# Second norm of a hybrid decoder layer: its small products get fixed places between the large ones

## The chip, the cores and the metric

The kernel runs on one NeuronCore of a Trainium2 chip. The metric is the device time of one execution in microseconds. The engines are named as in the profile: PE (TensorE matmul), PEld (TensorE weight load), DVE (VectorE), ACT (ScalarE), POOL (GpSimd) and SP (SyncE, whose queue issues most transfers).

## The reference

One layer over a prompt of 2048 tokens and eight single-token samples, `D_MODEL` 1024, `D_FF` 2816, all float32. What surrounds the change, cut to its core:

```python
h = rmsnorm(x, g_mix) * (1.0 + scale_m) + shift_m          # first norm
proj = h @ w_in                                            # q, k, v, gate, two LRU branches
...                                                        # retention heads, RG-LRU block
mix = jnp.concatenate([ret_out, lru_out], axis=-1) @ w_out # output projection
x = x + gate_m * mix

h = rmsnorm(x, g_ffn) * (1.0 + scale_f) + shift_f          # second norm
u = h @ w_up_conv
gv = h @ w_up_gate
uc, s_conv_ffn_new = causal_dwconv(u, s_conv_ffn, conv_ffn_w, conv_ffn_b)
f = (jax.nn.gelu(uc) * gv) @ w_down
x = x + gate_f * f
```

`rmsnorm` divides each token's row by the root of its mean square; then a final norm gives the output.

## The kernel before, in words

The 2056 columns (2048 tokens and 8 samples) are worked in three groups, each cut into two blocks of 344 or 340 columns (688 with the samples in the last group). Activations lie with features on the partitions, eight tiles of 128 features (`KC` = 8), and tokens along the free axis. Every large product is made three times in reduced float32: high part by high part, high by low, low by high (`mm3`; its three matmuls are lines 373, 374 and 375 in the profile). A "product" here is twelve such matmuls of 128 x 128 by 344 columns.

The program is a list of items (`group_items`), each with the weight blocks that it needs, a rate and a function. The main loop fetches weight blocks a little ahead, runs the function, and then advances two lists of generators: `soon` (by the item's rate) and `bg`. Instructions are traced in this order; a planner that models the engines' times then orders each engine's queue by readiness and priority. `urgent` wraps a generator so that its instructions get a priority ahead of their place. PSUM has two pools: `psm` with three banks and `pst` with five.

The end of a group's first half is the output projection `out_((2, 3), apart, 2)`: eight items for the first block, one for each feature tile, then eight for the second. An item makes one product (`down_item`, tile `down`), and VectorE adds it, scaled, to `x` (line 851). ScalarE squares each new tile of `x` (line 873) and VectorE adds the squares up (line 877); the last square of a block stays apart. Then `norm2` of the block is put into `soon`:

- the sums over features: for each piece of 128 tokens two small products, of the running sum and of the last square, with a column of ones (tile `bc`, line 888);
- mean and epsilon on VectorE (line 892), the power -1/2 on POOL (894), one diagonal tile for each piece on VectorE (897);
- the broadcast of the factor to all partitions by a product of ones and the diagonal tile (899);
- the operands of the FFN: `operands1` for the first block (`scaled` at line 913 and `hilo` at 923 and 924, tile by tile), `operands2` for the second.

The FFN's up-projections are made by a Strassen scheme with seven products on 2 x 2 halves. The two token blocks are its column halves. `PRODUCTS` names for each product the weight part and the operand: P1 takes `b11` and P2 `b21`, which come from the first block alone; P5 takes `t1`, P6 `t2`, P3 `b22`, P7 `t3`, P4 `t4`, which need the second block too. The accumulating PSUM banks are called `qx`, `qy` and `qz`. A quad is one such set for one pair of feature tiles and one of `w_up_conv` and `w_up_gate`. After the output projection come the P1 and P2 of quad 0 for both matrices, then the P1 and P2 of three further quads (`early`), then the rest of quad 0, in the order P5, P6, P3, P7, P4. `keep` copies a bank out of PSUM (`p`, line 1016, or with an addition line 1101).

Before the next group, `norm1` of that group makes its diagonal tiles (line 564) and broadcasts them (line 566).

Of the kernel before, what the change touches and what calls it, by code (L numbers as in the profile page):

```python
# [2 lines left out]

# [1 line left out]

# [9 lines left out]
ALU = mybir.AluOpType  # L15

P = 128
D = 1024
KC = D // P
# [79 lines left out]
def hybrid_step(ctx: ExitStack, tc: tile.TileContext, I, O):  # L99
# [35 lines left out]
    def tiny(cols, name):  # L135
        if cols == P:
            return sp.tile([P, P], F32, tag="wide", name=name, bufs=WIDE)
        return sp.tile([P, cols], F32, tag=name, name=name, bufs=1 if cols > 32 or name[:3] == "sp_" else None)
# [10 lines left out]
    ident = cst[:, C_ID:C_ID + P]  # L149
# [116 lines left out]
    units = {}  # L266
# [74 lines left out]
    def fetch_operand(key, lo_on):  # L341
# [25 lines left out]
        if (i == 1 or i == 2 and kind == "w_up_conv") and nm in ("A11", "A12"):  # L367

            del pr[nm]

    def mm3(out, wh, wl, xh, xl, first, last, more=False):

        T.matmul(out, wh, xh, start=first, stop=False, skip_group_check=more)  # L373
        T.matmul(out, wh, xl, start=False, stop=False, skip_group_check=more)  # L374
        T.matmul(out, wl, xh, start=False, stop=last, skip_group_check=more)  # L375

    ada_ps = {}

# [53 lines left out]
    def urgent(gen, offset=HASTE):  # L432

        while True:
            with tc.high_priority(offset=offset):
                try:
                    next(gen)
                except StopIteration:
                    return
            yield  # L440
# [33 lines left out]
    class Group:  # L474
# [83 lines left out]
        def norm1(g, b, how):  # L558
            bc = pst("bc") if g.gi else psm("bc")
            for i, (c0, w) in enumerate(g.pieces):  # L560
                a0, a1 = max(c0, b[0]), min(c0 + w, b[1])
                if a0 < a1:
                    dg = tiny(P, "dg")
                    V.tensor_scalar(out=dg[0:w, 0:a1 - a0], in0=ident[0:w, a0 - c0:a1 - c0],
                                    scalar1=g.r1[i][0:w, 0:1], scalar2=None, op0=ALU.mult)
                    T.matmul(bc[:, a0 - b[0]:a1 - b[0]], ones[0:w, :], dg[0:w, 0:a1 - a0],
                             start=True, stop=True)
            yield
            yield from g.hnorm(b, bc, 1, 0, how)
# [272 lines left out]
        def down_item(g, keys, parts, jg, b, m):  # L842

            np_, n = g.npr(b), b[1] - b[0]
            q = psm("down")
            for i, key in enumerate(keys):
                wh, wl = (v[:, m % 4, :] for v in units[key])
                xh, xl = parts[i][b]
                mm3(q[:, 0:n], wh, wl, xh, xl, i == 0, i == len(keys) - 1)
            xs = g.xk(m)[:, b[0]:b[0] + np_]  # L850
            V.scalar_tensor_tensor(out=xs, in0=q[:, 0:np_], scalar=modv[:, jg, m, 0:1], in1=xs,  # L851
                                   op0=ALU.mult, op1=ALU.add)
            if np_ < n:
                if (jg, m) not in g.started:
                    g.started.add((jg, m))
                    V.tensor_copy(fsv[:, m, :], q[:, np_:n])
                else:
                    V.tensor_tensor(out=fsv[:, m, :], in0=fsv[:, m, :], in1=q[:, np_:n], op=ALU.add)
# [19 lines left out]

        def norm2(g, b):
            n = b[1] - b[0]  # L880
            acc, sq = g.sq.pop(b)
            bc = pst("bc2")
            z = bc[:, 512 - 16:512]

            pcs = [(i, min(i, n - P), min(P, n - i)) for i in range(0, n, P)]
            for i, (_, r0, _) in enumerate(pcs):
                for a in (acc, sq):
                    T.matmul(z[:, 2 * i:2 * i + 2], a[:, r0:r0 + P], ones[:, 0:2],
                             start=(a is acc), stop=(a is sq))
            ss = tiny(8, "ss2")  # L890
            k = len(pcs)
            V.tensor_scalar(out=ss[:, 0:k], in0=z[:, 0:2 * k].rearrange("p (i t) -> p i t", t=2)[:, :, 0],
                            scalar1=1.0 / D, scalar2=EPS, op0=ALU.mult, op1=ALU.add)
            G.tensor_tensor(out=ss[:, 4:4 + k], in0=ss[:, 0:k], in1=mhalf[:, 0:k], op=ALU.pow)
            for i, (c0, r0, w) in enumerate(pcs):
                dg = tiny(P, "dg")
                V.tensor_scalar(out=dg[:, 0:w], in0=ident[:, c0 - r0:c0 - r0 + w],
                                scalar1=ss[:, 4 + i:5 + i], scalar2=None, op0=ALU.mult)
                T.matmul(bc[:, c0:c0 + w], ones, dg[:, 0:w], start=True, stop=True)
            yield  # L900
            yield from (g.operands1 if b == g.blocks[0] else g.operands2)(b, bc)

# [24 lines left out]
        def operands1(g, b, bc):  # L927
            g.n = n = b[1] - b[0]
            g.op = {v: slot("op", F32R) for v in ("b11", "b21")}
            g.keep32 = slot("keep")  # L930
            for k in range(KC):
                g.scaled(k, b[0], n, bc, g.raw32(k))
                g.hilo("b11" if k < 4 else "b21", k % 4, g.raw32(k), modv[:, 3, k, 0:1])
                yield

        def raw32(g, k):
# [65 lines left out]
        def product(g, st, key, nm, bank, start, tile):  # L1002

            wh, wl = units.pop(key)
            if start:
                st[bank] = tile("q" + bank)
            q = st[bank][:, 0:g.n]
            for k in range(4):
                mm3(q, wh[:, k, :], wl[:, k, :], g.hi(nm, k), g.lo(nm, k), start and k == 0, k == 3, not start)
            return q  # L1010

        def keep(g, q, name, more=None, pool=None):
# [8 lines left out]
        def quad_item(g, st, kind, i, what, out, apart):  # L1021

            left, right, bank, start = PRODUCTS[what]
            if apart:
                bank = "y" if what in ("P1", "P2") else bank
                start = what in ("P1", "P5", "P6")
            q = g.product(st, (kind, i, left), right, bank, start,
                          psm if bank == "y" and i < 3 else pst)
            p1 = st.get("p1")
            if what == "P1":  # L1030
                st["p1"] = g.keep(q, "p1", pool=fp if i == 1 else None)
            elif what == "P5":
                st["p5"] = g.keep(q, "p5", p1 if apart else None)
            elif what == "P6":
                st["u2"] = g.keep(q, "u2", p1 if apart else None)
            elif what == "P2":
                out(2 * i, 0, q, None if apart else st.pop("p1"))
            elif what == "P7":
                out(2 * i + 1, 1, q, st.pop("p5"))
            elif what == "P3":  # L1040
                out(2 * i, 1, q, st.pop("u2"))
            else:
                out(2 * i + 1, 0, q, st.pop("p1") if apart else None)
# [151 lines left out]
    def group_items(g, nxt):  # L1195
# [3 lines left out]
        def add(keys, rate, fn, *a):  # L1199
            out.append((keys, rate, fn, a))  # L1200
# [20 lines left out]
        def out_(ps, order, rate):  # L1221

            rows_, its, had = [512 * i + P * p for p in ps for i in range(2)], [], None

            def item(b, m, ks, norm):
                while any(b not in g.mixt.get(q, {}) for p in ps for q in (p, 4 + p)):
                    advance(bg)
                g.down_item(ks, [g.mixt[q] for p in ps for q in (p, 4 + p)], 2, b, m)
                if not norm:
                    return  # L1230
                if g.npr(b) < b[1] - b[0]:
                    g.gate_samples(2, m, 1)
                past = g.past.setdefault(b, [])
                past.append(m)
                if len(past) > 1:
                    g.square(b, past[-2], False)
                if len(past) == KC:
                    g.square(b, m, True)
                    soon.append(urgent(g.norm2(b)))

            for b, m in order:
                ks = [("w_out", a, m // 4) for a in rows_]
                its.append(([] if had == m // 4 else ks, rate, item, (b, m, ks, H - 1 in ps)))
                had = m // 4
            return its

        quads = {}

        def quad(kind, i, what, rate=1):
            st = quads.setdefault((kind, i), {})  # L1250
# [31 lines left out]
        lru(2)  # L1282
        lru(3)
        head(3, True)
        out.extend(out_((2, 3), apart, 2))
        its, out[n:] = out[n:], []

        ahead = [(kind, 0, nm) for kind in (UP, GATE)
# [3 lines left out]
        for it in its:  # L1292
            out.append(it)
            due += 0.45 * min(it[1], 1)
            if ahead and due >= 1:
                due -= 1
                key = ahead.pop(0)
                add([key], 0, units.pop, key)
        for kind in (UP, GATE):
            for what in ("P1", "P2"):  # L1300
                quad(kind, 0, what, 3)
        for what in ("P1", "P2"):
            for kind, i in early:
                quad(kind, i, what, 3)
        add([], 0, lambda: drain(soon))
        for pair in (("P5",), ("P6",), ("P3",), ("P7", "P4")):
            for kind in (UP, GATE):
                for what in pair:
# [144 lines left out]
```

## Time and profile before

| | |
|---|---|
| median of 3 runs | 2462.89 us (2462.57 to 2464.89) |
| profiled execution, its own time | 2463.86 us |
| its span | 2462.1 us |
| mean granted TensorE clock | 0.988 |
| PE busy | 2359.8 us (96%) |
| PEld busy | 2275.5 us (92%) |
| DVE busy | 1452.9 us (59%) |
| ACT busy | 869.6 us (35%) |
| POOL busy | 716.9 us (29%) |
| moved by DMA | 536.04 MB, mean 218 GB/s |

Busy time is counted inside the span, from the first to the last instruction of the profiled execution. Matmuls are pipelined: a record lasts about 0.32 us, while the next one starts about 0.16 us after it. A row of the trace's timeline gives the start, the length, engine, line, operation, tile written and tiles read, and in brackets how long the engine stood idle before it and what released it.

### The profile page before, as it was taken

What the parts mean: (1) busy time and instruction counts of PE and PEld (TensorE: products, weight loads), DVE (VectorE), ACT (ScalarE), POOL (GpSimd) and SP (SyncE); (2) the same over time, 40 slices, a digit from 0 to 9 for tenths busy, and PEclk for the clock granted to TensorE, in tenths of its full rate; (3) what the DMA queues carried; (4) which work ended last, traced back from release to release, by engine and by line L of the source; (5) the groups of instructions that cost most, each with busy time, mean ns of one, the idle gap of its engine ahead of it and who ended that gap; (6) DMA issues with size and microseconds to landing.
All of it is one profiled execution on the core that took longest, in us unless ns stands there. A gap on an engine that the chain in (4) does not pass through costs nothing.

```text
span 2462.1 us, 40114 instructions
## 1 busy us (share of the span) xinstructions
PE 2359.8 (96%) x15157; PEld 2275.5 (92%) x15157; DVE 1452.9 (59%) x3181; ACT 869.6 (35%) x1964; POOL 716.9 (29%) x739
## 2 busy tenths in 40 slices
PE   5999998999999999999899999999999989999998
PEld 4987797999999999999899999999999989999998
DVE  5646777875766665666754444446667675444444
ACT  4323554544444444243422222243124241222222
POOL 3444440257666743243001010112222210101011
PEclk9999999999999999999999999999999999999999
DMA  9476655878878875343566666666442465666674
GB/s 299 163 261 223 210 172 190 305 276 287 304 285 304 323 251 184 120 157 139 189 222 235 222 238 220 241 213 215 139 130 96 145 231 199 239 220 234 219 252 160
DMA packets 243493, 536.04 MB, mean 218 GB/s; under 512 B 19223, under 2 KB 114055, under 8 KB 243292
## 3 DMA queue, kind: packets, MB, share of 16 engines
q1 hardware_dynamic: 242220, 532.01, 62.6%
q8 instruction: 120, 1.97, 0.3%
q10 hardware_dynamic: 696, 0.91, 0.1%
q0 software_dynamic: 384, 0.56, 0.1%
q14 instruction: 73, 0.60, 0.1%
HBM read 385.10 MB, written 148.42 MB: 217 GB/s over the span
## 4 chain that ended last, share of the span: by engine, by line
PE 53%; DVE 4%; ACT 2%; DMA 1%; issue 1%; POOL 1%; POOLq 0%; SPq 0%; ACTq 0%; DVEq 0%
PE down L374 6%; PE down L373 6%; PE down L375 6%; PE qx L374 4%; PE qx L375 4%; PE qx L373 4%; PE proj L373 3%; PE proj L375 3%; PE proj L374 3%; PE qz L373 2%; PE qz L374 2%; PE qz L375 2%; PE qy L374 1%; PE qy L373 1%; PE qy L375 1%
## 5 line engine op out<-in xcount | busy, mean ns | idle before, releaser
L851 DVE SCALAR_TENSOR_TENSOR x<-down,mod,x 128x344 f32<-128x344 f32 (+2 forms) x624 | 349.0, 569 | 347.0 <-PE down L375 342.3
L373 PE MATMUL proj<-hh,wb 128*128 128x344 f32 (+1 forms) x1152 | 378.5, 329 | 14.3 <-DVE h L580 6.0
L375 PE MATMUL proj<-hh,wb 128*128 128x344 f32 (+1 forms) x1152 | 373.6, 325 | 2.7 <-POOL wb L304 2.5
L374 PE MATMUL proj<-hl,wb 128*128 128x344 f32 (+1 forms) x1152 | 372.5, 323 | 0.0
L458 POOL TENSOR_TENSOR ffl<-cv,ffh 128x344 fp32r<-128x344 f32 (+1 forms) x120 | 124.7, 1046 | 782.0 <-ACT ffh L457 736.7
L374 PE MATMUL qx<-op,wb 128*128 128x344 f32 (+1 forms) x1020 | 325.5, 319 | 2.6 <-DVE op L921 2.6
L373 PE MATMUL qx<-op,wb 128*128 128x344 f32 (+1 forms) x1020 | 324.7, 320 | 1.2 <-ACT op L920 1.2
L375 PE MATMUL qx<-op,wb 128*128 128x344 f32 (+1 forms) x1020 | 324.5, 319 | 0.0
L373 PE MATMUL down<-ffh,wb 128*128 128x344 f32 (+1 forms) x960 | 304.7, 324 | 7.6 <-DVE x L851 7.4
L375 PE MATMUL down<-ffh,wb 128*128 128x344 f32 (+1 forms) x960 | 306.4, 319 | 0.0
L374 PE MATMUL down<-ffl,wb 128*128 128x344 f32 (+1 forms) x960 | 306.3, 319 | 0.0
L304 POOL TENSOR_TENSOR wb<-wr,wb 128x512 fp32r<-128x512 f32 x164 | 223.9, 1376 | 230.7 <-ACT wb L303 222.1
L373 PEld LDWEIGHTS proj<-hh,wb 128*128 128x128 f32 x1152 | 218.4, 190 | 25.9 <-issue 9.5
L375 PEld LDWEIGHTS proj<-hh,wb 128*128 128x128 f32 x1152 | 218.7, 190 | 5.7 <-POOL wb L304 3.9
L374 PEld LDWEIGHTS proj<-hl,wb 128*128 128x128 f32 x1152 | 219.1, 190 | 3.3 <-POOL hl L588 0.9
L1076 DVE SCALAR_TENSOR_TENSOR cv<-u,vec,cv 128x344 f32<-128x344 f32 (+2 forms) x264 | 170.8, 665 | 50.6 <-ACT cv L1056 48.1
L374 PEld LDWEIGHTS qx<-op,wb 128*128 128x128 f32 x1020 | 191.7, 188 | 3.4 <-DVE op L921 3.4
L373 PEld LDWEIGHTS qx<-op,wb 128*128 128x128 f32 x1020 | 191.5, 188 | 2.0 <-ACT op L920 1.8
L373 PEld LDWEIGHTS down<-ffh,wb 128*128 128x128 f32 x960 | 179.3, 188 | 14.3 <-DVE x L851 13.7
L375 PEld LDWEIGHTS qx<-op,wb 128*128 128x128 f32 x1020 | 191.4, 188 | 0.0
L373 PE MATMUL qz<-op,wb 128*128 128x344 f32 (+1 forms) x528 | 169.7, 325 | 14.6 <-ACT op L920 10.7
L375 PEld LDWEIGHTS down<-ffh,wb 128*128 128x128 f32 x960 | 180.6, 188 | 0.0
(314 smaller groups left out, 4952.1 us busy)
## 6 DMA issues: line engine op xcount, KB each, us to landing
wb<-w_down SPq DMA_DIRECT2D x100, 512.0 KB
wb<-w_up_conv_S SPq DMA_DIRECT2D x92, 512.0 KB
wb<-w_up_gate_S SPq DMA_DIRECT2D x92, 512.0 KB
wb<-w_in SPq DMA_DIRECT2D x72, 512.0 KB
wb<-w_up_conv_A SPq DMA_DIRECT2D x69, 512.0 KB
wb<-w_up_gate_A SPq DMA_DIRECT2D x69, 512.0 KB
w_in<-wb SPq DMA_DIRECT2D x48, 512.0 KB
w_up_conv_S<-wb SPq DMA_DIRECT2D x44, 512.0 KB
```

The lines of the kernel that those rows point to most:

```text
L304: lo_on.tensor_tensor(out=w[:, 512:1024], in0=src, in1=w[:, 0:512].bitcast(F32), op=ALU.subtract)
L373: T.matmul(out, wh, xh, start=first, stop=False, skip_group_check=more)
L374: T.matmul(out, wh, xl, start=False, stop=False, skip_group_check=more)
L375: T.matmul(out, wl, xh, start=False, stop=last, skip_group_check=more)
L458: G.tensor_tensor(out=lo[:, 0:n], in0=src, in1=hi[:, 0:n].bitcast(F32), op=ALU.subtract)
L851: V.scalar_tensor_tensor(out=xs, in0=q[:, 0:np_], scalar=modv[:, jg, m, 0:1], in1=xs, op0=ALU.mult, op1=ALU.add)
L1076: V.scalar_tensor_tensor(out=cv[:, 0:np_], in0=u[:, j:j + np_], scalar=cfw[:, j, ft:ft + 1], in1=cv[:, 0:np_], op0=ALU.mult, op1=ALU.add)
```

## The change

1. All eight squares of a block go into one running sum on VectorE, so the sums take one small product for each piece of 128 tokens.
2. `norm2` no longer goes into `soon` but into a list of its own, `chain`, advanced by step items at given positions: its sums stand after one more product, its broadcast after another, and then one operand tile is made with each item. The rate of the output projection's items goes from 2 to 1.
3. Ordering edges without a semaphore (`issue_after`) tie the small products behind the last large product traced (`last_mm`), all later large products of `down_item` and `product` behind the last small product (`hold`), the operand instructions on VectorE (and the first norm's diagonal tiles) behind the last addition to `x` (`last_add`), and the first products on `t1` behind the last early product.
4. The early products come by halves: P1 of quad 0 for both matrices, then P2 of both, then the six early ones. For the second block the sums stand after the first P1, the broadcast after the second, and the operand steps after the others, three for each.
5. The `qy` bank of quad 0 comes from `pst` instead of `psm`.

```diff
+    last_mm, last_add, hold = [None], [None], [None]
+    def behind(ref):
+        return tc.issue_after(ref[0].ins) if ref[0] is not None else nullcontext()
...
-        T.matmul(out, wl, xh, start=False, stop=last, skip_group_check=more)
+        last_mm[0] = T.matmul(out, wl, xh, start=False, stop=last, skip_group_check=more)
... norm1
-                    V.tensor_scalar(out=dg[0:w, 0:a1 - a0], in0=ident[0:w, a0 - c0:a1 - c0],
-                                    scalar1=g.r1[i][0:w, 0:1], scalar2=None, op0=ALU.mult)
+                    with behind(last_add):
+                        V.tensor_scalar(out=dg[0:w, 0:a1 - a0], in0=ident[0:w, a0 - c0:a1 - c0],
+                                        scalar1=g.r1[i][0:w, 0:1], scalar2=None, op0=ALU.mult)
... down_item
-            for i, key in enumerate(keys):
-                wh, wl = (v[:, m % 4, :] for v in units[key])
-                xh, xl = parts[i][b]
-                mm3(q[:, 0:n], wh, wl, xh, xl, i == 0, i == len(keys) - 1)
+            with behind(hold):
+                for i, key in enumerate(keys):
+                    wh, wl = (v[:, m % 4, :] for v in units[key])
+                    xh, xl = parts[i][b]
+                    mm3(q[:, 0:n], wh, wl, xh, xl, i == 0, i == len(keys) - 1)
...
-            V.scalar_tensor_tensor(out=xs, in0=q[:, 0:np_], scalar=modv[:, jg, m, 0:1], in1=xs,
-                                   op0=ALU.mult, op1=ALU.add)
+            last_add[0] = V.scalar_tensor_tensor(out=xs, in0=q[:, 0:np_], scalar=modv[:, jg, m, 0:1], in1=xs,
+                                                 op0=ALU.mult, op1=ALU.add)
... norm2
-            acc, sq = g.sq.pop(b)
+            acc, = g.sq.pop(b)
...
-            for i, (_, r0, _) in enumerate(pcs):
-                for a in (acc, sq):
-                    T.matmul(z[:, 2 * i:2 * i + 2], a[:, r0:r0 + P], ones[:, 0:2],
-                             start=(a is acc), stop=(a is sq))
+            with behind(last_mm):
+                for i, (_, r0, _) in enumerate(pcs):
+                    hold[0] = T.matmul(z[:, 2 * i:2 * i + 2], acc[:, r0:r0 + P], ones[:, 0:2], start=True, stop=True)
...
+            dgs = []
             for i, (c0, r0, w) in enumerate(pcs):
-                dg = tiny(P, "dg")
-                V.tensor_scalar(out=dg[:, 0:w], in0=ident[:, c0 - r0:c0 - r0 + w],
+                dgs.append(tiny(P, "dg"))
+                V.tensor_scalar(out=dgs[i][:, 0:w], in0=ident[:, c0 - r0:c0 - r0 + w],
                                 scalar1=ss[:, 4 + i:5 + i], scalar2=None, op0=ALU.mult)
-                T.matmul(bc[:, c0:c0 + w], ones, dg[:, 0:w], start=True, stop=True)
+            yield
+            with behind(last_mm):
+                for i, (c0, r0, w) in enumerate(pcs):
+                    hold[0] = T.matmul(bc[:, c0:c0 + w], ones, dgs[i][:, 0:w], start=True, stop=True)
             yield
... operands1
-                g.scaled(k, b[0], n, bc, g.raw32(k))
-                g.hilo("b11" if k < 4 else "b21", k % 4, g.raw32(k), modv[:, 3, k, 0:1])
+                with behind(last_add):
+                    g.scaled(k, b[0], n, bc, g.raw32(k))
+                    g.hilo("b11" if k < 4 else "b21", k % 4, g.raw32(k), modv[:, 3, k, 0:1])
... product
-            for k in range(4):
-                mm3(q, wh[:, k, :], wl[:, k, :], g.hi(nm, k), g.lo(nm, k), start and k == 0, k == 3, not start)
+            with behind(hold), behind(last_mm if nm == "t1" and key[1] == 0 else [None]):
+                for k in range(4):
+                    mm3(q, wh[:, k, :], wl[:, k, :], g.hi(nm, k), g.lo(nm, k), start and k == 0, k == 3, not start)
... quad_item
-                          psm if bank == "y" and i < 3 else pst)
+                          psm if bank == "y" and 1 <= i < 3 else pst)
... out_
-                    g.square(b, m, True)
-                    soon.append(urgent(g.norm2(b)))
+                    g.square(b, m, False)
+                    chain.append(urgent(g.norm2(b)))
...
+        def steps(n):
+            add([], 0, lambda: [advance(chain) for _ in range(n)])
...
-        out.extend(out_((2, 3), apart, 2))
+        for i, it in enumerate(out_((2, 3), apart, 1)):
+            out.append(it)
+            if i >= KC:
+                steps(2 if i == KC + 1 else 2 if i == 2 * KC - 1 else 1)
...
-        for kind in (UP, GATE):
-            for what in ("P1", "P2"):
-                quad(kind, 0, what, 3)
-        for what in ("P1", "P2"):
-            for kind, i in early:
-                quad(kind, i, what, 3)
-        add([], 0, lambda: drain(soon))
+        first = [(kind, 0, what) for what in ("P1", "P2") for kind in (UP, GATE)]
+        first += [(kind, i, what) for what in ("P1", "P2") for kind, i in early]
+        for n, v in enumerate(first):
+            quad(*v)
+            steps(1 if n < 2 else 3)
+        add([], 0, lambda: drain(chain))
```

More of the change, by code (lines that the diff above doesn't have):

```diff
@@ L1 @@
 import math
-from contextlib import ExitStack
+from contextlib import ExitStack, nullcontext
 import numpy as np
@@ L1245, in out_ @@
             return its
-        quads = {}
+        chain, quads = [], {}
+        def steps(n):
+            add([], 0, lambda: [advance(chain) for _ in range(n)])
         def quad(kind, i, what, rate=1):
```

## The prediction

> **What bounds the kernel now.** I read the page first, then TensorE's idle time by windows, then its waits, then the instructions in order of time around the second norm.
>
> ```profile
> span 2462.1 us, 40114 instructions
> PE 2359.8 (96%) x15157; PEld 2275.5 (92%) x15157; DVE 1452.9 (59%) x3181; ACT 869.6 (35%) x1964; POOL 716.9 (29%) x739
> ```
>
> TensorE (PE) is the bound: only 102 us of the span are idle, and nothing else is above 59%. A change can win only idle PE time, PE time at reduced clock, or PE work. The three stretches from the last output-projection product of a group to the end of its first FFN products, one per token group:
>
> ```profile
> 386.00:431.80 45.80, 34.53 (x189) 31.99 (x187) 37.05 (x83) 19.81 (x47) 3.76 (x2) 0.89 0.57 201
> 1188.00:1232.40 44.40, 37.11 (x213) 35.12 (x212) 34.03 (x77) 19.00 (x51) 4.62 (x3) 0.92 0.64 224
> 1974.00:2016.80 42.80, 35.65 (x212) 34.05 (x213) 33.97 (x97) 21.51 (x54) 3.80 (x3) 0.96 0.61 215
> sum 133.00, PE 107.29 PEld 101.16 DVE 105.04 ACT 60.33 POOL 12.18; mean PE 35.76 PEld 33.72 DVE 35.01 ACT 20.11 POOL 4.06
> ```
>
> Columns: window, length, busy PE, PEld, DVE, ACT, POOL, then granted clock, DMA share, GB/s. PE is idle 133.00 - 107.29 = 25.7 us here, a quarter of its idle time in 5% of the span. Who ends it (engine, line, released by: total us, times, longest):
>
> ```profile
> PE qz L373 <- ACT op L920: 10.7, 3, 6.3
> PE qy L373 <- ACT p L1016: 4.0, 3, 1.7
> PE qz L373 <- ACT p L1016: 3.6, 3, 2.1
> PE qx L374 <- DVE op L921: 2.6, 3, 1.2
> PE qx L373 <- ACT op L920: 1.2, 1, 1.2
> PE qy L374 <- DVE op L924: 1.1, 2, 0.6
> PE bc L888 <- DVE sq L877: 1.0, 1, 1.0
> PE qz L374 <- DVE op L921: 0.8, 2, 0.5
> ```
>
> These are 25.0 of the 25.7 us. The first is the first product on `t1`: after the second block's broadcast PE has nothing placed to run while the operand is made. In the second group:
>
> ```profile
> 1188.06 0.32 PE L373 MATMUL qy<-op,wb 128*128 128x340 f32 x1
> 1194.59 1.40 PE L888 MATMUL bc<-ones,sq 128*128 128x2 f32 x12
> 1195.84 0.40 PE L373 MATMUL qx<-op,wb 128*128 128x340 f32 x1
> 1199.68 0.79 PE L899 MATMUL bc<-dg,ones 128*128 128x128 f32 x6
> 1202.20 0.58 PE L373 MATMUL qz<-op,wb 128*128 128x340 f32 x2 [1.73 <-ACT op L920]
> ```
>
> Three early products run, then the sums, two more products (3.84 us for two: 1.9 each), the broadcast, a 1.73 us hole. The other early products come after `t1`'s, when they cover nothing. The clock also drops:
>
> ```profile
> 404.00:414.00 10.00, 6.92 (x28) 0.66 0.26 95
> 421.00:427.00 6.00, 5.60 (x26) 0.72 0.37 124
> 1203.00:1209.00 6.00, 5.87 (x27) 0.72 0.02 5
> 1227.00:1232.00 5.00, 5.00 (x23) 0.66 0.67 210
> 1988.00:1994.00 6.00, 5.45 (x23) 0.72 0.06 20
> ```
>
> (Window, length, busy PE, clock, DMA share, GB/s.) Length times (1 - clock) is the loss: 1.7 us in each of the last four. The first has 3.4, part of it under idle; I take 2.5.
>
> **The change part by part.**
>
> *Sums.* The last square joins the others on VectorE, so each piece needs one small product, not two. 12 records took 1195.84 - 1194.59 = 1.25 us, 0.104 each; 6 norms lose 6 each: **-3.75 us** of PE work. VectorE gains 6 additions of 0.5 us; they lengthen the way to the sums and are counted in the waits below. POOL's power steps stay six.
>
> *Products by halves, `t1` last.* Between the second block's broadcast and the first `t1` product now stand eight early products, 8 x 1.9 = 15 us. The operand needed 1.7 to 6.3 us. Its waits go: 10.7 + 0.8 = **-11.5**; the reduced clock behind them goes with them: 2.5 + 1.7 + 1.7 = **-5.9**. The ten weight blocks are the same in another order; SP's queue carries no transfer more, and 512 KB per 1.9 us asks 277 GB/s, so I looked at what the stretch before the broadcast already moved:
>
> ```profile
> 1181.60:1200.40 18.80, 17.75 (x116) 17.06 (x115) 13.25 (x34) 6.31 (x13) 0.85 (x1) 1.00 0.77 283
> 1200.40:1225.00 24.60, 19.78 (x109) 18.20 (x108) 24.35 (x52) 13.77 (x36) 2.87 (x1) 0.93 0.48 162
> ```
>
> 283 GB/s at a DMA share of 0.77: weights keep up, cost nothing; without that cover each late block is PE idle.
>
> *Waits ahead of the sums* (1.1, 1.0 and the 0.7 not listed): **-2.8**; the new waits take their place.
>
> *Later waits.* `p` and `qx`: 4.0 + 3.6 + 2.6 + 1.2 = 11.4, and two clock drops of 1.7: 14.8 together. VectorE is busy 24.35 of 24.60 us after the broadcast: it sets the pace there. With 15 us of products in front it gains on PE, and the quad-0 `y` bank moves to the pool of five; but the ScalarE copies `p` still stand in one queue behind operand copies that wait for VectorE. Bounds 0 and -14.8; nothing in the trace decides, I take half: **-7.4**.
>
> *Fixed places.* Today PE passes a late sum by; now the products are tied behind it. 12 places: sums and broadcast, twice a group. Where the sums ran (first) and the broadcast, for the first block of each group:
>
> ```profile
> 370.82 0.28 PE L888 MATMUL bc<-ones,sq 128*128 128x2 f32 x2
> 378.72 0.80 PE L899 MATMUL bc<-dg,ones 128*128 128x128 f32 x6
> 1173.56 0.28 PE L888 MATMUL bc<-ones,sq 128*128 128x2 f32 x2
> 1180.79 0.61 PE L899 MATMUL bc<-dg,ones 128*128 128x128 f32 x4
> 1958.38 0.32 PE L888 MATMUL bc<-ones,sq 128*128 128x2 f32 x2
> 1962.87 0.61 PE L899 MATMUL bc<-dg,ones 128*128 128x128 f32 x4
> ```
>
> Distances 7.9, 7.2 and 4.5 us; by the new places two products and half a sum, about 4.5. So VectorE gets the first block's operands 3.4, 2.7 and 0 us earlier. The second block's sum is the critical one. Where PE left the output projection, and VectorE's last square sum:
>
> ```profile
> 386.04 0.40 PE L373 MATMUL qy<-op,wb 128*128 128x344 f32 x1
> 1974.19 0.39 PE L373 MATMUL qy<-op,wb 128*128 128x344 f32 x1 [0.50 <-DVE gs L866]
> 393.72 0.52 DVE L877 TENSOR_TENSOR sq<-sq 128x344 f32<-128x344 f32 x1
> 1191.67 1.13 DVE L877 TENSOR_TENSOR sq<-sq 128x340 f32<-128x340 f32 x2
> 1976.38 2.38 DVE L877 TENSOR_TENSOR sq<-sq 128x344 f32<-128x344 f32 x4
> 404.16 0.69 DVE L357 TENSOR_TENSOR ws<-ws,wr 128x512 f32<-128x512 f32 x1 [5.42 <-DMA wr<-in_w_up_conv]
> ```
>
> VectorE lagged 8.2, 4.7 and 5.1 us (393.72 + 0.52 - 386.04, and so on; the third from 1973.7). The place gives it 1.9, the added sum costs 0.5, so an unchanged lag waits 6.8, 3.3 and 3.7 = 13.8; with free engines (add 0.6, square 0.5, sum 0.5 and gaps: about 2) some 0.2 each. Since VectorE's work is the same but begins earlier, I take the lag less the head start: 3.4, 0.6, 3.7 = 7.7. The other nine places are within some tenths of a product: 1.1. Two of the waits pass the 1.73 that was enough for a clock drop; I take one, 1.7. **+10.5** in all, bounds 1.7 and 13.8 + 1.1 + 5.1 = 20.
>
> *VectorE's own DMA wait.* At 404.16 it stood 5.42 us for a raw weight with ready operand work queued behind. That can recur; now 15 us of products lie over it. Bounds 0 and 5.4, I take **+1**, nearer to the covered case.
>
> *First norm's diagonal tiles behind the last addition.* They leave the second norm's neighbourhood for the group change:
>
> ```profile
> L564 DVE TENSOR_SCALAR dg<-cst,r x21: 228/282/290, 18.8 to 1200.1; 128x128 f32<-128x128 f32 x12, 128x88 f32<-128x88 f32 x2, 128x40 f32<-128x40 f32 x2, 48x48 f32<-48x48 f32 x2
> ```
>
> Seven of 0.28 us, twice: 0 to 3.9; I take **0**, since the output products of that place run beside them. Rate 2 to 1 and the empty step items issue nothing.
>
> Sum: -3.75 - 11.5 - 5.9 - 2.8 - 7.4 + 10.5 + 1 = -19.9. The profiled execution took 2463.86 (span 2462.1 and 1.8 around it), so 2444.0; the median of the runs, 2462.89, lies 1.0 below it: **2443 us**. All low ends give 2426, all high ends 2468.
>
> [...]
>
> **The rivals.**
>
> *The lag stays.* If VectorE puts the operand passes ahead of the squares, the second block's sums wait 13.8 and each costs a clock drop: 20 instead of 10.5, so 2452.5. For it: the wait of 5.42 us above, with ready work behind. Against: the head start in two groups. [...]
>
> *The later waits go wholly* and the sums wait 6 instead of 10.5: 2443 - 7.4 - 4.5 = 2431. For it: 15 us ahead for a VectorE that needs 24. Against: `p` copies were late by their queue, not by work.
>
> *Slower: VectorE decides every place.* If backlog stands ahead of sums and of diagonal tiles alike, 12 places at w us each: without the 10.5 the sum is -30.4, so it turns slower from w = 2.5, or 2.1 with clock drops. At w = 3 and six drops: -30.4 + 36 + 10 = +16, 2479 us. For it: additions, square sums and operand passes are four instructions per item, at 24.35 / 52 = 0.47 each some 1.9 us of VectorE for 1.9 of PE. Against: at the broadcasts the chain (sum, power, three tiles) took less than the two products that stood there.
>
> *The order comes out as now.* Only the records go: 2459.5. Against: two products between sum and broadcast would have to stay.
>
> **How the numbers follow.** Forecast 0.46 (2436 to 2450), lag stays 0.22, later waits gone 0.18, order as now 0.07, slower 0.07. What differs by less than 0.2% (4.9 us) cannot be told from no change here. Faster takes the first three but for a tenth of the second: 0.84; same 0.09; slower 0.07. The range 2430 to 2457 leaves out slower, most of order as now and the low end of later waits gone.
>
> **What would show it.** Right: L888's records 72 to 36, square sums 42 to 48; about 96 matmuls between the second broadcast and the first `qz`; the `qz` <- ACT `op` wait gone; idle in the three stretches 25.7 down to about 17; a new wait of `bc` on `sq`. Wrong: waits of 3 us and more at L888 in every group, new DMA waits of PE, or the waits on `p` grown by what `t1`'s lost.

## The result, and the profile after

| | before | after |
|---|---|---|
| median | 2462.73 us (2459.01 to 2464.89) | 2440.64 us (2435.96 to 2444.45) |
| ratio | | 0.9921, 95% interval 0.9898 to 0.9944 |
| profiled execution, its own time | 2463.86 us | 2444.45 us |
| span, mean granted clock | 2462.1 us, 0.988 | 2442.7 us, 0.986 |

The change wins 22 us by the medians, 19.5 us by the ratio, and 19.4 us between the two profiled executions, which is the difference that follows here; the one of after is the slowest of its four. Of all executions in this document one, of the kernel "nothing held" below, took 4633.02 us at a clock of 1.0; why is not shown, and it is left out there. New line numbers: `mm3` 379 to 381, addition to `x` 859, square sum 885, sums 896, broadcast 910, `scaled` 924, `hilo` 931 to 935, copy `p` 1030. The head of the page of after:

```profile
span 2442.7 us, 40060 instructions
PE 2352.9 (96%) x15121; PEld 2275.2 (93%) x15121; DVE 1468.4 (60%) x3187; ACT 873.1 (36%) x1964; POOL 722.5 (30%) x739
```

PE's idle time fell from 2462.1 - 2359.8 = 102.3 to 2442.7 - 2352.9 = 89.8 us (-12.5), its busy time by 6.9. To see where, both executions are cut at the same events: last out-projection product, first `w_down` product, last FFN product, first product of the next group. The windows view, first before, then after (window, length, busy PE, PEld, DVE, ACT, POOL with their counts, clock, DMA share, GB/s). The rows are, in order, the first stretch behind the output projection, the first group's FFN, the second stretch, the third group's first half up to the stretch, and the third stretch:

```profile
386.00:443.65 57.65, 46.23 (x261) 43.41 (x259) 45.40 (x96) 27.10 (x65) 7.53 (x5) 0.91 0.63 220
443.65:853.32 409.67, 401.13 (x2517) 394.33 (x2515) 286.49 (x425) 190.21 (x435) 253.86 (x194) 1.00 0.82 296
1188.06:1243.47 55.41, 48.12 (x285) 46.13 (x283) 38.93 (x87) 22.75 (x61) 5.54 (x4) 0.94 0.67 225
1667.91:1973.50 305.59, 299.83 (x1983) 287.28 (x1981) 204.31 (x546) 92.28 (x184) 79.29 (x115) 0.99 0.43 143
1973.50:2027.99 54.49, 47.02 (x285) 45.24 (x284) 40.51 (x114) 25.49 (x65) 4.74 (x4) 0.97 0.67 230
```

```profile
384.75:437.04 52.29, 46.68 (x278) 45.62 (x277) 44.42 (x90) 31.22 (x75) 6.89 (x6) 0.93 0.75 258
437.04:840.53 403.49, 396.90 (x2491) 390.60 (x2491) 294.83 (x422) 188.49 (x426) 261.00 (x192) 1.00 0.84 298
1171.20:1216.48 45.28, 43.16 (x278) 42.40 (x277) 35.36 (x79) 23.55 (x62) 3.72 (x4) 1.00 0.82 277
1637.85:1955.10 317.25, 306.88 (x1993) 294.13 (x1992) 208.58 (x568) 96.02 (x193) 80.47 (x116) 0.97 0.41 137
1955.10:2008.66 53.56, 47.33 (x272) 46.48 (x271) 38.06 (x104) 25.40 (x63) 3.75 (x4) 0.90 0.67 230
```

Lengths change by -5.4, -6.2, -10.1, **+11.7** and -0.9 us. Read the counts too: the first stretch holds 17 matmuls more than before and the FFN behind it 26 fewer. At some 0.16 us each, about 4 of the FFN's 6.2 us is work that now runs in the stretch. Those two rows therefore belong together: -11.5 us, of which 5.8 + 2.0 = 7.8 is idle time. The second stretch loses 7.29 - 2.12 = 5.2 us of idle and all of its reduced clock (0.94 before, 1.00 after). The row that got longer is the surprise: 4.6 us more idle (5.76 to 10.37), and a lower clock (0.99 before, 0.97 after). The stretches between these rows make up the other -8.5 us: 4.0 in the second group's first half, 3.1 in the change to the third group, 1.3 in the first group's first half.

In the prediction's own three windows, idle went from 25.7 to 116.80 - 103.38 = 13.4 us:

```profile
sum 116.80, PE 103.38 PEld 101.00 DVE 98.59 ACT 65.20 POOL 7.71; mean PE 34.46 PEld 33.67 DVE 32.86 ACT 21.73 POOL 2.57
```

Who ends PE's idle time in after (engine, line, released by: total us, times, longest); there is no row of `qz` waiting for `op` any more:

```profile
PE bc L896 <- DVE sq L885: 8.6, 3, 4.1
PE qz L379 <- ACT p L1030: 4.6, 3, 1.9
PE oT L681 <- DVE on L477: 2.1, 1, 2.1
PE qx L379 <- DVE p L1115: 0.5, 1, 0.5
PE qy L379 <- ACT p L1030: 0.3, 1, 0.3
```

And the places themselves in after's timeline, the second block's sums of each group, and the broadcast and the first product on `t1` of two:

```profile
390.35 1.44 PE L896 MATMUL bc<-ones,sq 128*128 128x2 f32 x6 [3.70 <-DVE sq L885]
395.24 1.42 PE L910 MATMUL bc<-dg,ones 128*128 128x128 f32 x6
411.94 0.32 PE L379 MATMUL qz<-op,wb 128*128 128x344 f32 x1
1173.89 0.83 PE L896 MATMUL bc<-ones,sq 128*128 128x2 f32 x6 [0.81 <-DVE sq L885]
1176.54 0.79 PE L910 MATMUL bc<-dg,ones 128*128 128x128 f32 x6
1192.42 0.32 PE L379 MATMUL qz<-op,wb 128*128 128x340 f32 x1
1960.29 1.44 PE L896 MATMUL bc<-ones,sq 128*128 128x2 f32 x6 [4.08 <-DVE sq L885]
```

Between broadcast and `t1` lie 15 us of early products, and `t1` starts without a bracket, so without a wait. The sums now wait instead. Why 3.70 us in the first group shows VectorE's queue just ahead of them:

```profile
385.62 0.57 DVE L859 SCALAR_TENSOR_TENSOR x<-down,mod,x 128x344 f32<-128x344 f32 x1
386.11 1.05 DVE L924 SCALAR_TENSOR_TENSOR keep<-x,mod,bc 128x344 f32<-128x344 f32 x2
...
388.59 1.28 DVE L304 TENSOR_TENSOR wb<-wr,wb 128x512 fp32r<-128x512 f32 x2
389.79 0.51 DVE L885 TENSOR_TENSOR sq<-sq 128x344 f32<-128x344 f32 x1
```

Between the last addition and the last square sum, VectorE still works on operands of the first block and on weight splits (`wb`, three of some 0.65 us).

### The profile page after: what moved, and what is told of

It reads as the page before. It is cut to its first block, busy times and chain, and to the rows that moved or that the text cites. A ratio compares the mean times of both kernels' runs of the same rounds, so it can differ in the third digit from the quotient of the medians.

```text
span 2442.7 us, 40060 instructions
## 1 busy us (share of the span) xinstructions
PE 2352.9 (96%) x15121; PEld 2275.2 (93%) x15121; DVE 1468.4 (60%) x3187; ACT 873.1 (36%) x1964; POOL 722.5 (30%) x739
## 4 chain that ended last, share of the span: by engine, by line
PE 54%; DVE 5%; ACT 2%; issue 1%; POOL 1%; DMA 0%; POOLq 0%; SPq 0%; ACTq 0%; DVEq 0%
PE down L380 6%; PE down L381 6%; PE down L379 6%; PE qx L380 4%; PE qx L381 4%; PE qx L379 4%; PE proj L379 4%; PE proj L381 3%; PE proj L380 3%; PE qz L379 2%; PE qz L381 2%; PE qz L380 2%; PE qy L379 1%; PE qy L380 1%; PE qy L381 1%
## 5 line engine op out<-in xcount | busy, mean ns | idle before, releaser
L379 PEld LDWEIGHTS down<-ffh,wb 128*128 128x128 f32 x960 | 179.4, 188 | 12.1 <-DVE x L859 11.4
L380 PEld LDWEIGHTS down<-ffl,wb 128*128 128x128 f32 x960 | 180.5, 188 | 0.0
```

## The experiments

My theory: the gain is cover. Products that need nothing new now lie over the making of `t1`, and what the change gives back sits at two kinds of place, the second block's sums and one late first-block sum in the third group. The rivals: the gain lies in the single sum, in the diagonal tiles, in the order by halves or in one of the ties; or VectorE sets the pace, whatever the places. The bank of item 5 and the rate of item 2 were not tried by themselves.

Each kernel was timed beside executions of before of its own (medians 2461.02, 2461.51 and 2462.04 us in three sets), and after was not timed again with them. By the intervals of the ratios, a distance to after of less than about 0.0027, some 7 us, is not told apart from none.

**One sum alone, on the kernel before.**

```diff
-                for a in (acc, sq):
-                    T.matmul(z[:, 2 * i:2 * i + 2], a[:, r0:r0 + P], ones[:, 0:2], start=(a is acc), stop=(a is sq))
+                T.matmul(z[:, 2 * i:2 * i + 2], acc[:, r0:r0 + P], ones[:, 0:2], start=True, stop=True)
```

> Kernel before, with the last square in the running sum and one small product for each piece, nothing else. Theory: 36 records of 0.104 us go, 3.75 us, less what the added sum costs where PE waits for it (0.5 us in the first group): 2459 to 2461. Rival: the shorter sums let the planner reorder much and are the main part of the gain: 2450 or less.

2456.86 us, 0.9983 (0.9973 to 0.9994): 4.2 us, a fifth of the change. The wait for `t1` stays, but it is 4.5 us shorter than before's 10.7, all of it in the first group (a hole of 1.74 us where before had 6.25). So the 4.2 us need not be the 36 records alone. Waits of PE:

```profile
PE qz L373 <- ACT op L918: 6.1, 3, 2.7
```

**First norm's diagonal tiles alone, on the kernel before.** Only `with behind(last_add):` around line 564.

> Kernel before, with the first norm's diagonal tiles behind the last addition to x and nothing else. Theory: they cost and bring nothing: 2461 within 2. Rival: they free buffers early and account for part of the gain outside the three stretches (6 us in the first group's FFN, 4 and 3 us around the second group change): 2450 to 2456.

2461.18 us, 1.0002 (0.9992 to 1.0013): nothing.

**The cover taken away, all else kept.** The second block's sums stand behind the eighth early product, so `t1`'s operand starts when little is left to run over it.

```diff
-            steps(1 if n < 2 else 3)
+            steps(0 if n < 7 else 1 if n < 9 else 3)
```

> Changed kernel, with the second block's sums seven products later (after eight early products, the broadcast after nine, one product in front of t1). Theory: it is the cover of t1 that makes the gain: the wait of t1 on ACT op and DVE op comes back (11.5 us before, less one product for each group: 5 to 8 us) and clock drops behind it, while the sums wait for nothing: 2438 to 2446, and 10 us or more above the version with the sums two products later. Rival: the gain is from the shorter sums and from what the planner does elsewhere; the cover does not matter: within 4 us of the version with the sums two later, and no wait of qz on op.

2463.36 us, 1.0009 (1.0 to 1.0019). The whole gain is gone, with single sum, ties and order by halves in place. The waits on `t1` are back, tile by tile, and a long one for a bank has joined:

```profile
PE qz L380 <- DVE op L932: 6.7, 10, 1.1
PE qz L379 <- ACT op L931: 5.2, 3, 1.7
PE qy L379 <- ACT p L1030: 3.9, 1, 3.9
```

It lost 17 us more than the upper end that I expected, but in the direction and at the place that the theory names: the gain needs the products that lie over the making of `t1`. Between the profiles of after and of this kernel PE's idle time rose by 8.1 us (89.8 to 97.9) and its busy time by 12.5, with a mean clock of 0.982 for 0.986. The edit also moves everything that VectorE makes for the second block, so the 23 us are not the price of `t1`'s wait alone.

**One product later.** The other way along the same scale: the sums get one more product ahead.

```diff
-            steps(1 if n < 2 else 3)
+            steps(0 if n < 1 else 1 if n < 3 else 3)
```

> Changed kernel, with the second block's sums one product later (after two early products, the broadcast after three). Theory: VectorE's backlog makes the sums late by up to 4.1 us; a product of 1.9 us in front takes 1.9 + 0.8 + 1.9 of the 8.6 us of PE waits and with them some clock drops: 5 to 9 us less, about 2434. Rival: VectorE is the bound of the stretch, so the wait reappears at the first t1 product or later: 2441 within 3.

2431.49 us, 0.9881 (0.9863 to 0.9898), 9 us better than the change itself (0.0040 by the ratios). Its waits, and its three stretches by windows cut as above:

```profile
PE bc L896 <- DVE sq L885: 4.0, 2, 2.2
```

```profile
383.35:431.40 48.05, 45.12 (x278) 44.26 (x277) 45.81 (x93) 30.57 (x75) 7.11 (x6) 0.96 0.80 278
1160.64:1203.90 43.26, 42.73 (x277) 42.28 (x276) 35.22 (x78) 23.56 (x61) 3.70 (x4) 1.00 0.84 291
1938.78:1989.80 51.02, 46.16 (x276) 45.35 (x275) 40.23 (x108) 26.21 (x65) 3.65 (x4) 0.93 0.74 252
```

They add up to 142.33 us against 52.29 + 45.28 + 53.56 = 151.13 in after, 8.8 us less. The two profiled executions are 19.1 us apart, since after's is its slowest and this one (2425.33) the fastest of its five: 6.3 us of idle time and 13.0 of busy time, with a clock of 0.993 for 0.986. So the three stretches account for less than half of what these two traces differ by, and that 8.8 is near the 9 us of the medians is no proof. What the waits do show is that the place right behind the first product was too early: 8.6 us at the sums became 4.0.

**Two products later.**

```diff
+            steps(0 if n < 2 else 1 if n < 4 else 3)
```

> Changed kernel, with the second block's sums two products later (after three early products, the broadcast after four; six products stay in front of t1). Theory: of the sums' wait only the largest (4.0 us one product later: two groups) is left, so 2 to 5 us less than one product later: about 2428; t1 still starts without a wait, since 6 x 1.9 = 11 us of products cover 2 to 6 us. Rival: the backlog moves along and shows at t1 or at the p copies: 2431 to 2434.

2447.43 us, 0.994 (0.9925 to 0.9955): a miss. It is 16 us behind one product later; from the change itself, 5 us better by the ratios, it is not told apart. The sums hardly wait (0.3 us), but `t2`, the operand after `t1`, is now late:

```profile
PE qx L379 <- ACT op L931: 10.7, 3, 3.6
```

The program makes the operands on VectorE one after another behind the sum, so moving the sum moves them all; after has no such row. The places trade a wait at the sum (8.6 us in after) for waits at the later operands (10.7 us here); the best of the four tried is one product later.

**The first block's small products hold nothing back.** In the third group they stand behind an out-projection product that needs the last retention head, and all later products are tied behind them:

```diff
+                    mm = T.matmul(...)
+                    hold[0] = mm if b != g.blocks[0] else hold[0]
...
```

(The same for the broadcast.)

> Changed kernel, but the first block's small products no longer hold the later large products back (they keep their places behind the product before them). Theory: in the third group the sums stand behind an item that waits for the retention's tail, and all other items are tied behind the sums, so PE idles and the clock drops (that stretch grew by 11 us against before). Untied, the stretch shrinks by 6 to 11 us: about 2432 (2428 to 2436). Rival: the tail itself is late whatever PE may run, and the tie is harmless: 2441 within 3.

2446.35 us, 0.9947 (0.9931 to 0.9962): 6 us above the change, at the edge of what can be told, where a gain of 5 to 13 us was expected. The end of the third group's first half in after's timeline, then the same 25 us or so by windows in before, after and this kernel:

```profile
1932.75 0.40 PE L681 MATMUL oT<-cst,on 80*128 80x80 f32 x1 [2.15 <-DVE on L477]
1934.00 0.65 PE L379 MATMUL down<-mix,wb 128*128 128x344 f32 x1 [0.85 <-ACT mix L463]
1936.60 1.27 PE L896 MATMUL bc<-ones,sq 128*128 128x2 f32 x6
```

```profile
1948.00:1973.50 25.50, 25.12 (x171) 23.70 (x163) 20.24 (x62) 7.50 (x16) 4.09 (x8) 1.00 0.38 133
```

```profile
1930.00:1955.00 25.00, 21.66 (x115) 20.84 (x114) 15.93 (x55) 6.47 (x13) 2.58 (x4) 0.80 0.24 89
```

```profile
1929.40:1954.40 25.00, 23.27 (x153) 22.52 (x153) 18.33 (x62) 6.81 (x14) 4.14 (x8) 1.00 0.34 117
```

The diagnosis of the place was right: without the tie PE has other products for most of the 2.15 us hole (0.6 is left), the clock stays at 1.00, and 153 matmuls fit where 115 did. That is some 3 us of idle and 25 x 0.20 = 5 of clock, and the third group's first half takes 307.75 us here, 9.5 less than after's 317.25: most of the +11.7 row above. But the tie also brought the first block's broadcast early. In the first group it starts 5.51 us after its sums here (371.96 and 377.47), and 2.65 us in after. VectorE's operands of that block need the broadcast, so they start later, and the second block's sums paid in all three groups:

```profile
PE bc L896 <- DVE sq L885: 16.1, 3, 7.6
```

**Both: first block free and sums one product later.**

> Both edits of the two runs before together. Theory: the two losses are at different places and add up: 12 to 18 us less than the changed kernel, about 2426. Rival: one of them only moves the wait: about 2433; both only move it: 2441.

2434.57 us, 0.9901 (0.9883 to 0.9919), not told apart from one product later alone. The two do not add up: the wait at the sums is 10.1 us, where one product later alone had 4.0.

**One product later, and the third group's first sums one item later.**

```diff
-            if i >= KC:
-                steps(2 if i == KC + 1 else 2 if i == 2 * KC - 1 else 1)
+            if i >= KC + g.last:
+                steps(2 if i == KC + 1 + g.last else 2 + g.last if i == 2 * KC - 1 else 1)
```

> The version with the second block's sums one product later (2431), and in the third group alone the first block's sums and broadcast one item later. Theory: in that group the sums stand behind an item that waits for the retention's tail (idle 2.15, 0.86 and 0.33 us in a row and 3 to 8 us lost to the clock behind it); one more item in front gives PE something to run there: 3 to 6 us less, about 2427. Rival: the operands of the third group start later and the second block's sums wait longer by as much: 2431 within 2.

2430.21 us, 0.988 (0.9866 to 0.9893): the lowest median, not told apart from one product later alone (2431.49). The hole for the head is still there (1.6 us), and the sums wait 4.6.

**Nothing held.** `hold` is never set; large products may pass the small ones, as before.

> Changed kernel, with the small products still behind the large product before them but holding nothing back. Theory: the tie pulls the first block's broadcast forward and so VectorE's whole chain; without it PE runs other products first, as with the first block freed (2446): 2444 to 2452. Rival: the planner fills the sums' waits with other products and the time falls: 2432 to 2438.

0.9953 (0.9939 to 0.9966), and a median of 2449.4 us over the eight executions that are left (2450.46 with the ninth): holding is worth 8 to 9 us. The time was expected, the reason was not. PE passes the late sum and then stops for banks that ScalarE has not emptied:

```profile
PE qy L379 <- ACT p L1030: 16.1, 3, 9.9
```

**Operands not tied behind the last addition.** No `behind(last_add)` in `operands1`.

> Changed kernel, with the first block's operand instructions on VectorE no longer tied behind the last addition to x. Theory: VectorE's backlog ahead of the second block's square sums sets the largest new wait; untied, the eight operand tiles go in one lump ahead of additions and squares, so the sums (8.6 us of waits in three groups) wait 5 to 10 us more, with clock drops: 2446 to 2453. Rival: the work is the same and only its order differs; the sums wait as long: 2441 within 3.

2446.9 us, 0.9936 (0.992 to 0.9951). The wait at the sums rose by 1.3 us only, to 9.9, less than I gave it. Its executions (2440.23 to 2447.8) overlap those of after, and the ratios are 0.0015 apart: that this tie gains anything is not shown.

**`t1` not tied; and the products not by halves.** The first takes `behind(last_mm ...)` off `product`; the second restores the old order:

```diff
-        first = [(kind, 0, what) for what in ("P1", "P2") for kind in (UP, GATE)]
+        first = [(kind, 0, what) for kind in (UP, GATE) for what in ("P1", "P2")]
```

> Changed kernel, with the first t1 products no longer tied behind the last early product. The planner then puts the first of them some 34 matmuls (three products) sooner. Theory: five products, 9.5 us, still cover the 2 to 6 us that the operand needs after the broadcast: 2441 within 3, the wait of qz on op at most 1 us. Rival: the tie is what makes the gain: 2447 or more.

> Changed kernel, with the four products of quad 0 in the order before (P1 and P2 of the one matrix, then of the other); the sums stand after the first, the broadcast after the second as they do now. Theory: P2 needs the first block's last four operand tiles, which VectorE makes last, so the product between sums and broadcast may wait some tenths for each group; otherwise the same places and the same cover: 2441 to 2444. Rival: the halves matter by the order of the weights: 2447 or more.

2443.57 us, 0.9926 (0.9911 to 0.9941), and 2440.96 us, 0.9912 (0.9895 to 0.9929). Neither is told apart from the change, and `qz` waits for no `op` in either: by themselves these two parts bring nothing that these runs can show.

## Why the prediction was right, point by point

Split by kind, the predicted sum of -19.9 was -10.2 of idle time (-11.5 - 2.8 + 7.7 + 1.1 - 5.7 + 1), -5.9 of clock and -3.75 of work. Measured between the profiles: -12.5 of idle and -6.9 of busy time, which is -3.75 of work, if the records cost what the forecast took, and -3.1 of clock and whatever else makes PE busy. Two figures do not follow from the prediction's own terms. Idle time of "about 17" in the three stretches would be 25.7 - 10.2 = 15.5 by these terms. And "2.1 with clock drops" counts three drops, where the sentence behind it counts six; with six it is (30.4 - 10.2) / 12 = 1.7.

- *Sums.* 72 records became 36 and the square sums 42 became 48, as said; the rows of the grouped view read as follows. Alone this gave 4.2 us for 3.75, with a shorter wait for `t1` in it.

```profile
L896 PE MATMUL bc<-ones,sq x36: 207/272/374, 370.1 to 1961.4; 128*128 128x2 f32 x36
L885 DVE TENSOR_TENSOR sq<-sq x48: 494/508/520, 358.6 to 2430.1; 128x344 f32<-128x344 f32 x34, 128x340 f32<-128x340 f32 x14
```

- *Products by halves, `t1` last.* The waits for `t1` went wholly, and 96 matmuls stand between the second broadcast and the first `qz` in each group, as said. That the cover is what keeps them away is shown by the kernel with the sums behind eight products, where they are back. But 4.5 of the 11.5 us may have gone without it: the first group's hole of 6.25 us came while VectorE stood 5.42 us for a raw weight, and with one sum alone and no cover it was 1.74. Why that wait was gone there is not shown. That "by halves" matters is not shown either: the old order is as fast.
- *Second block's sums.* Forecast 3.4, 0.6 and 3.7 us; measured 3.70, 0.81 and 4.08. The rival by which the lag stays put them at 13.8 together; it was 8.6. The agreement is partly luck, because the head start was mis-sized. The prediction put two products and half a sum, about 4.5 us, between the first block's sums and its broadcast, where item 2 of the change puts one product. In after the distances are 2.65, 2.65 and 4.72 us, the first as follows.

```profile
370.06 0.83 PE L896 MATMUL bc<-ones,sq 128*128 128x2 f32 x6
372.71 0.80 PE L910 MATMUL bc<-dg,ones 128*128 128x128 f32 x6
```

So, counted from the sums, VectorE could begin 5.2 and 4.6 us earlier and 0.2 later, not 3.4, 2.7 and 0 earlier, and "the lag less the head start" would give 1.6, 0 and 3.9 = 5.5 us for the 8.6 measured. The direction holds: with the first block free the distances are 5.51, 5.16 and 5.55 us and the waits 7.62, 3.23 and 5.21.

- *Later waits.* 5.4 us are left in the waits on `p` and `qx` of 11.4, and one clock drop of 1.7 behind the `qz` wait of 1.89 us: about half, as taken, though without a reason. What the bank from the pool of five has to do with it was not tried. The wait on a bank depends on the places too (16.1 us with nothing held).
- *The rivals.* Later waits gone wholly: 5.4 us are left. VectorE decides every place: PE waited for it at three of the twelve. The order as now: 15 us of products moved ahead of `t1`.
- *Diagonal tiles* 0: right, measured alone.
- *VectorE's DMA wait* of +1: no new wait of PE on a DMA appears, and VectorE's longest wait for a raw `w_up_conv` fell from 5.4 to 1.5 us.

Two more steps failed. **"The other nine places are within some tenths of a product"**: eight were; the third group's first sums stand behind the product that waits for the last head, and what is tied behind them waits too. I priced a place by whether its own operand was ready, and did not ask what the product just ahead of it was waiting for. **The clock drop behind the sums, 1.7 once**, was 3.4 twice: the windows of after around the first and the third group's sums, and the one around the late head, give 12 x 0.28 = 3.4, 23 x 0.15 = 3.4 and 18 x 0.28 = 5.0 us.

```profile
388.00:400.00 12.00, 9.65 (x46) 9.65 (x47) 7.89 (x18) 2.72 (x8) 0.85 (x1) 0.72 0.76 282
1953.00:1976.00 23.00, 18.92 (x105) 18.63 (x103) 15.45 (x52) 8.27 (x17) 0.85 (x1) 0.85 0.59 207
1928.00:1946.00 18.00, 14.66 (x72) 13.82 (x71) 8.65 (x29) 2.80 (x7) 2.58 (x4) 0.72 0.01 4
```

One row to see it by was there: the 6.3 us hole of before cost 3.4. So was a row against the premise that a hole of 1.73 us is enough for a drop, which was read from holes that had cost something. In the same group of before a second hole of 1.73 us cost nothing:

```profile
1216.39 0.42 PE L373 MATMUL qy<-op,wb 128*128 128x340 f32 x1 [1.73 <-ACT p L1016]
1216.00:1228.00 12.00, 9.52 (x59) 1.00 0.60 195
```

(The second row is of PE alone: window, length, busy PE, clock, DMA share, GB/s.) A hole of this size had no fixed price here, as the last section shows too, so the clock terms of the sum are what one execution lost and not what the next one must lose.

These misses, some 12 us together, were made up by less idle time in the three windows than the sum gives (13.4 us for 15.5) and by places that the sum did not name: the second group's first half (-4.0, mostly clock), the change to the third group (-3.1), the first FFN's own idle (-2.0) and the first group's first half (-1.3). That the total came out within 2.4 us of the median is partly luck. In the second group's first half both profiles have the same three holes (1.86, 1.83 and 2.92 us before, 1.86, 1.84 and 2.96 after). Each was followed by a clock of 0.86 over 12 us in before, only the first in after: 2 x 1.7 = 3.4 of the 4.0 us, with nothing in the holes themselves that changed. Why the other three places got shorter is not settled.

## What to carry to other kernels

A fixed place for a small product trades two waits: too early and the large engine stands at the place itself (8.6 us at the sums in after), too late and the operands made from it come behind their cover (10.7 us at `t2` with two products later). Here one product more ahead gained 9 us and a second one lost 16 again, so the place is worth trying at its neighbours. Before tying work behind a place, look at what the instruction just ahead of it waits for, because the tie passes that wait on to everything behind: with the first block free of it, the third group's first half was 9.5 us shorter here.

## What the runs showed of the hardware

Where a clock drop was measured behind a hole here, the loss was near 1.7 us, or two or three times that. Window times (1 - clock) is 10 x 0.17 = 1.7 behind a hole of 1.82 us (one product later), 12 x 0.14 = 1.7 behind 1.89 (after, the `qz` wait), 20 x 0.09 = 1.8 behind 3.60 (two products later) and 3.4 behind 3.70 and 4.08 (rows above); behind 0.81 it is nothing (clock 1.00). With the first block free, a hole of 3.23 us cost 16 x 0.11 = 1.8 and one of 7.62 cost 18 x 0.28 = 5.0; yet with the sums behind the eighth product 3.92 us cost 16 x 0.32 = 5.1, so in these profiles the longer hole did not always cost more.

Of the holes between 1.7 and 3 us some cost something and some nothing. The hole ahead of the first group's second sums was 1.82 us both with one product later and with the third group's first sums later too. The first cost 12 x 0.14 = 1.7 us, the second nothing (PE alone, columns as above):

```profile
388.95 1.04 PE L896 MATMUL bc<-ones,sq 128*128 128x2 f32 x6 [1.82 <-DVE sq L885]
388.00:400.00 12.00, 11.05 (x64) 0.86 0.97 360
```

```profile
390.96 0.83 PE L896 MATMUL bc<-ones,sq 128*128 128x2 f32 x6 [1.82 <-DVE sq L885]
390.00:402.00 12.00, 10.35 (x67) 1.00 0.98 359
```

A hole in the second group's first half (`zr`, waiting for `xc`) cost 1.7 us in before (2.92 us long, clock 0.86 over 12 us) and nothing in after (2.96, 1.00). From `zr` to the fourteenth `proj` matmul behind it PE took 4.74 us in before, 3.29 in after and, with `t1` not tied, 6.03 behind a hole of 2.95. So a few us of clock between two single profiles are no sign of what an edit does.

Behind the 3.70 us hole PE was busy 6.65 of 7.00 us and still had a clock of 0.52 (the row below); the matmuls between sums and broadcast started 0.29 us apart, those behind the broadcast 0.16. This stretch contains the two-column products of the sums (1.44 us for six); whether they make it longer was not tried by itself. Behind the 6.25 us hole of before, where none stood, the matmuls also started 0.29 us apart, with a few gaps, from 406.60 to about 412.2, which is 5.6 us, and 0.16 apart from there on.

```profile
390.00:397.00 7.00, 6.65 (x27) 6.65 (x28) 3.67 (x10) 1.07 (x3) 0.85 (x1) 0.52 0.78 289
```
